# Queries and keys of one map side by side: three pairs of digit operations per tile in place of six

## The chip, the cores and the metric

The kernel runs on 1 core of one Trainium2 chip. The metric is the device time of one execution in microseconds (us), as the median of several runs. Engines are named as in the profile: PE (TensorE's matmuls), PEld (its weight loads), DVE (VectorE), ACT (ScalarE), POOL (GpSimd), SP (SyncE, which issues most DMAs).

## The reference, cut to what matters

One encoder layer on 1024 tokens of width 1024, in float32. The part that the change touches is the differential attention: 8 heads, and in each head two softmax maps (the index `i`), each with its own queries and keys of width 64, over one value of width 128.

```python
z = h @ w_in[l]
q = z[..., POOL_DIM:POOL_DIM + QK_DIM].reshape(B, S, N_HEADS, 2, HEAD_DIM)
k = z[..., POOL_DIM + QK_DIM:POOL_DIM + 2 * QK_DIM].reshape(B, S, N_HEADS, 2, HEAD_DIM)
...
qn = head_rmsnorm(q, g_q) * (HEAD_DIM ** -0.5)
kn = head_rmsnorm(k, g_k)
...
    s = jnp.einsum('bqhid,bkhid->bihqk', qblk, kn)
...
    s = jnp.where(allowed, s + bias, neg)
    p = jax.nn.softmax(s, axis=-1)
    a = p[:, 0] - lam * p[:, 1]
    return jnp.einsum('bhqk,bkhe->bqhe', a, vf)
```

Around it stand a pooling mixer, two sigmoid gates from `h @ w_gate`, an output projection and a squared-ReLU MLP.

## The kernel before, in words

**Digits.** Every float32 operand of a matmul is split into two: a high digit, which is the value rounded to the matmul's float32r format, and a low digit, the remainder. `split` (L117) writes the high one with an ACT copy (L119) and the low one with a DVE or POOL subtraction (L120). `mm3` (L122) then makes three matmuls of a product: high by high (L125), high by low (L126), low by high (L127).

**Stages of the attention.** The work is cut by head h (8) and tile t of 128 tokens (8), so in 64 steps. For each step the code writes these stages:

- A, `stage_qkv`: 24 matmuls into `z`, 128 tokens by q (128 columns), k (128), v (128).
- B, `stage_prep`: squares (ACT, L422), their sums (DVE, L423), the power -0.5 (POOL, L234), the values' digits, the normalized q and k in `qn` (DVE, L427), and the gains on the key part (POOL, L433).
- C, `stage_qkT`: two transposes of `qn` on PE into the bank `tk`, then the digits of K and Q. For each map ACT copies the high digit of K (L454), DVE subtracts for the low one (L455), ACT copies the high digit of Q (L456), DVE subtracts twice (L457, L458), ACT copies once more (L459). High digits of a map lie on its own 64 partitions, low digits on the other 64, so that one matmul over 128 partitions adds two digit products.
- D, `stage_scores`: for each map two matmuls `sc` per 512 keys (L485, L486), the bias and running minimum on DVE (L488), the exponential on ACT (L496), then the difference of the two maps on DVE (L503 to L505).
- E, `stage_aT`: transposes `ta` of the result (L541) and their digits `AT`. F, `stage_pv`: the products `po` with the values. H, `stage_ssq`: the sums of squares of the output, by two matmuls (L576, L577). R, `stage_norm`: row factors of the head, with a transpose `trr` (L597).

**Fill.** The gates (`gate_cols`, 16 column blocks c of 2 halves, matmuls `g`) and the pooling mixer (`pool_group`, 4 groups of 2 halves, matmuls `u` and `yp`) don't depend on the attention and are written to stand among it. A half of a gate is 24 matmuls into one bank; ACT then moves the bank to memory (L731; for `u` L696, for `yp` L723).

**Banks.** PSUM has 8 banks, all in use: 2 for `z`, 2 for `sc`, 2 shared by `tk`, `ta` and `trr`, 1 for `po`, and 1, the pool `ps_f`, for the fill. Fill tiles thus follow each other in one bank, and the next can't start before ACT has emptied the last. Only from gate column 13 on (`G_Z`) does `spare_bank` take the two `z` banks too.

**What sets the order.** Each engine runs its own list of instructions in order. The lists are made when the kernel is built, by a scheduler that goes by the order of the code (the string at L50 and the loop at L631 for the attention; the fill is written behind it and has lower priority) and by its own model of how long each instruction takes. A change of shapes therefore changes the lists everywhere in the attention.

**After the attention** come the branch projections (`bp`, `baX`, `baY`), the output projection (`op`), the MLP's up side (`X`, `Y`, `Z`, `W`) and its down side (`Da`, `Db`).

Of the kernel before, what the change touches and what calls it, by code (L numbers as in the profile page):

```python
# [17 lines left out]
P = 128  # L18
# [39 lines left out]
def encoder_kernel(  # L58
# [215 lines left out]
    with ExitStack() as ph:  # L274
# [6 lines left out]
        def s1(shape, dt, name, tag, bufs=1):  # L281
            return sq_pool.tile(shape, dt, tag=tag, name=name, bufs=bufs)
# [133 lines left out]
        def stage_prep(h, t):  # L416
# [6 lines left out]
            nc.vector.tensor_reduce(ms, sq.rearrange("p (a b) -> p a b", a=4), axis=AX.X, op=ALU.add)  # L423
            rsq(ms, ms, 4, 1.0 / HD)
            split(V[th][:, t % 4, 0, :], V[th][:, t % 4, 1, :], z[:, 256:384])
            qn = s1([P, 4, HD], F32, f"qn{h}_{t}", "qn", N_QN)
            nc.vector.tensor_tensor(  # L427
                qn,
                z[:, 0:256].rearrange("p (a b) -> p a b", a=4),
                ms.unsqueeze(2).broadcast_to([P, 4, HD]),  # L430
                op=ALU.mult,
            )
            nc.gpsimd.tensor_tensor(  # L433
                qn[:, 2:4, :], qn[:, 2:4, :], ggh.unsqueeze(1).broadcast_to([P, 2, HD]), op=ALU.mult
            )
            st[h, t] = {"qn": qn}
            yield
# [1 line left out]
        def stage_qkT(h, t):  # L439

            th, c0 = t // 4, (t % 4) * P
            K, qn = KV[h][0][th], st[h, t]["qn"]
            tr = ps_t.tile([P, 512], F32, tag="tr", name=f"tk{h}_{t}")
            for i in range(2):
                nc.tensor.transpose(
                    tr[:, i * P : (i + 1) * P], qn[:, 2 * i : 2 * i + 2, :].rearrange("p a b -> p (a b)"), identf
                )
            Q = s1([P, 2, 2, P], F32R, f"Q{h}_{t}", "Q", N_Q)
            halves = (slice(0, HD), slice(HD, P))
            for m in range(2):  # L450
                own, other = halves[m], halves[1 - m]
                q, k = tr[own, 0:P], tr[own, P : 2 * P]
                k_hi, q_hi = K[own, m, c0 : c0 + P], Q[own, m, 0, :]
                nc.scalar.copy(k_hi, k)  # L454
                nc.vector.tensor_tensor(K[other, m, c0 : c0 + P], k, f(k_hi), op=ALU.subtract)  # L455
                nc.scalar.copy(q_hi, q)  # L456
                nc.vector.tensor_tensor(Q[other, m, 0, :], q, f(q_hi), op=ALU.subtract)  # L457
                nc.vector.tensor_tensor(Q[own, m, 1, :], q, f(q_hi), op=ALU.subtract)  # L458
                nc.scalar.copy(Q[other, m, 1, :], q)  # L459
            st[h, t]["Q"] = Q  # L460
            yield

# [1066 lines left out]
```

## Time and profile before

| | |
|---|---|
| median of 3 runs | 1535.6 us (1534.63 to 1535.61) |
| the profiled execution, its own time | 1535.99 us |
| its span, first to last instruction | 1534.0 us |
| PE busy | 1514.5 us, 99% |
| DVE, ACT, POOL busy | 69%, 54%, 21% |
| granted TensorE clock | 1.00 |
| attention, first `tk` to last `po` matmul | about 43 to 690 us |

The page of the profile sums each engine's busy time; a window gives the same for a stretch of the span. A line of the timeline is start, duration, engine, line of the code, operation and operands, and in brackets the idle time of the engine before it with what ended it. Matmuls are pipelined: a 128x512 matmul is shown with some 0.39 us, but the next one starts 0.23 us after it.

### The profile page before, as it was taken

To read this page: it belongs to the slowest core of one execution; us is meant where nothing else is said; L and a number is where in the kernel's file an instruction comes from. 1 tells how busy PE (TensorE), PEld (TensorE's weight loads), DVE (VectorE), ACT (ScalarE), POOL (GpSimd) and SP (SyncE) were. 2 spreads that over 40 slices of the span, in tenths; PEclk is the share of its full clock that TensorE was granted. 3 is DMA by queue.
4 is the path that set the end of the run, shared out by engine and by line. 5 is a ranking of instruction groups with operands and counts; after the bars stand their busy time and mean duration, and the time that the engine had idled before them with its cause. 6 is when DMAs were issued, how large, how long until landed. Compare 5 with 4: busy or idle time off the path is not lost.

```text
span 1534.0 us, 22224 instructions
## 1 busy us (share of the span) xinstructions
PE 1514.5 (99%) x7601; PEld 1311.1 (85%) x7601; DVE 1063.2 (69%) x2358; ACT 825.3 (54%) x1821; POOL 329.4 (21%) x476
## 2 busy tenths in 40 slices
PE   7999999999999999999999999999999999999999
PEld 6999999899999999888888888888888888888887
DVE  6777776777778887845578549766665668556572
ACT  6666565656566566554465456565555634333331
POOL 6654563333334243312000111000000000000000
PEclk9999999999999999999999999999999999999999
DMA  7331321110202021626466634454333799537760
GB/s 243 112 119 52 107 95 57 53 60 31 83 23 90 17 77 63 240 76 242 149 199 215 225 111 137 166 184 158 138 138 110 256 357 372 179 124 260 226 193 28
DMA packets 171611, 221.11 MB, mean 144 GB/s; under 512 B 10901, under 2 KB 104810, under 8 KB 171498
## 3 DMA queue, kind: packets, MB, share of 16 engines
q1 hardware_dynamic: 154090, 192.39, 38.0%
q10 hardware_dynamic: 17408, 27.30, 4.8%
q8 instruction: 60, 0.98, 0.3%
q14 instruction: 53, 0.43, 0.1%
HBM read 157.76 MB, written 61.90 MB: 143 GB/s over the span
## 4 chain that ended last, share of the span: by engine, by line
PE 92%; DVE 3%; DMA 3%; SPq 1%; issue 1%; ACT 1%; POOL 0%; DVEq 0%; ACTq 0%
PE z L125 5%; PE z L127 5%; PE z L126 5%; PE Da L125 4%; PE Da L126 4%; PE Da L127 4%; PE g L125 3%; PE g L127 3%; PE g L126 3%; PE Db L126 3%; PE Db L125 3%; PE Db L127 3%; PE X L127 3%; PE X L126 3%; PE X L125 3%; PE sc L485 2%
## 5 line engine op out<-in xcount | busy, mean ns | idle before, releaser
L125 PE MATMUL z<-wqkv,hT 128*128 128x384 f32 x512 | 174.5, 341 | 0.1
L126 PE MATMUL z<-wqkv,hT 128*128 128x384 f32 x512 | 174.0, 340 | 0.0
L127 PE MATMUL z<-wqkv,hT 128*128 128x384 f32 x512 | 173.8, 340 | 0.0
L496 ACT ACTIVATE s<-s,nm 128x256 f32<-128x256 f32 (+7 forms) x128 | 99.7, 779 | 77.0 <-DVE nm L488 69.2
L125 PE MATMUL g<-hT,fwgate 128*128 128x512 f32 x256 | 100.8, 394 | 0.9 <-ACT go L731 0.9
L126 PE MATMUL g<-hT,fwgate 128*128 128x512 f32 x256 | 100.6, 393 | 0.0
L127 PE MATMUL g<-hT,fwgate 128*128 128x512 f32 x256 | 100.3, 393 | 0.0
L125 PEld LDWEIGHTS z<-wqkv,hT 128*128 128x128 f32 x512 | 96.6, 189 | 3.6 <-DVE qn L427 0.3
L126 PEld LDWEIGHTS z<-wqkv,hT 128*128 128x128 f32 x512 | 96.7, 189 | 3.2
L127 PEld LDWEIGHTS z<-wqkv,hT 128*128 128x128 f32 x512 | 96.6, 189 | 2.4 <-DVE hT L120 0.5
L234 POOL TENSOR_TENSOR ms<-ms,mhalf 128x4 f32<-128x4 f32 x64 | 67.4, 1053 | 128.7 <-DVE ms L233 113.5
L488 DVE CUSTOM_DVE_ANT_0 s<-sc,dist 128x512 f32<-128x512 f32 (+3 forms) x128 | 74.8, 585 | 13.4 <-PE sc L486 11.4
L120 DVE TENSOR_TENSOR AS<-s,AS 128x512 fp32r<-128x512 f32 x64 | 44.1, 692 | 35.8 <-ACT AS L119 35.7
L485 PE MATMUL sc<-K,Q 128*128 128x512 f32 (+2 forms) x192 | 67.2, 359 | 0.3 <-DVE nm L488 0.3
L120 POOL TENSOR_TENSOR wqkv<-rqkv,wqkv 128x384 fp32r<-128x384 f32 x60 | 62.6, 1057 | 13.1 <-ACT wqkv L119 9.7
L486 PE MATMUL sc<-K,Q 128*128 128x512 f32 (+2 forms) x192 | 65.1, 353 | 0.0
L459 ACT CAST Q<-tk 64x128 fp32r<-64x128 f32 x128 | 33.3, 260 | 50.7 <-DVE Q L458 48.4
L456 ACT CAST Q<-tk 64x128 fp32r<-64x128 f32 x128 | 33.2, 259 | 50.8 <-DVE K L455 49.4
L433 POOL TENSOR_TENSOR qn<-qn,ggh 128x128 f32<-128x128 f32 x64 | 31.4, 491 | 115.4 <-DVE qn L427 88.6
L125 PEld LDWEIGHTS g<-hT,fwgate 128*128 128x128 f32 x256 | 48.1, 188 | 9.3 <-ACT go L731 1.5
L127 PEld LDWEIGHTS g<-hT,fwgate 128*128 128x128 f32 x256 | 48.1, 188 | 8.8
L126 PEld LDWEIGHTS g<-hT,fwgate 128*128 128x128 f32 x256 | 48.1, 188 | 8.2
(475 smaller groups left out, 4651.8 us busy)
## 6 DMA issues: line engine op xcount, KB each, us to landing
wd<-in_w_down_dram SPq DMA_DIRECT2D x56, 512.0 KB, 5.9
wu<-in_w_up_dram SPq DMA_DIRECT2D x32, 512.0 KB, 4.5
udS<-us SPq DMA_DIRECT2D x64, 256.0 KB, 2.4
ur<-udS SPq DMA_DIRECT2D x32, 512.0 KB, 3.5
rqkv<-in_w_in_dram SPq DMA_DIRECT2D x64, 192.0 KB, 2.9
ud<-u ACTq DMA_DIRECT2D x48, 256.0 KB, 4.3
ur<-ud SPq DMA_DIRECT2D x24, 512.0 KB, 4.8
frgate<-in_w_gate_dram SPq DMA_DIRECT2D x32, 256.0 KB, 2.9
```

The lines of the kernel that those rows point to most:

```text
L120: return (lo_eng or nc.vector).tensor_tensor(lo, src, f(hi), op=ALU.subtract)
L125: nc.tensor.matmul(ps, lhs_hi, rhs_hi, start=first, stop=False, **kw)
L126: nc.tensor.matmul(ps, lhs_hi, rhs_lo, start=False, stop=False, **kw)
L127: nc.tensor.matmul(ps, lhs_lo, rhs_hi, start=False, stop=last, **kw)
L234: nc.gpsimd.tensor_tensor(dst, dst, mhalf[:, :n], op=ALU.pow)
L433: nc.gpsimd.tensor_tensor(qn[:, 2:4, :], qn[:, 2:4, :], ggh.unsqueeze(1).broadcast_to([P, 2, HD]), op=ALU.mult)
L456: nc.scalar.copy(q_hi, q)
L459: nc.scalar.copy(Q[other, m, 1, :], q)
L485: nc.tensor.matmul(dst, Q[:, i, 0, :], rhs, start=True, stop=False)
L486: nc.tensor.matmul(dst, Q[:, i, 1, :], rhs, start=False, stop=True)
L488: nc.vector.tensor_tensor_reduce(out=s[i][:, c : c + w], in0=sc[:, 0:w], in1=dist[:, o0 + c : o0 + c + w], scale=2.0 ** -(h + 1), scalar=B ...
L496: nc.scalar.activation(s[i][:, 0:n], s[i][:, 0:n], AF.Exp, bias=last, scale=-1.0, accum_out=Z[:, i, t : t + 1])
```

## The change

In `stage_prep` the normalized tile `qn` is laid out map by map: q of map 0, k of map 0, q of map 1, k of map 1 (before: both q, then both k). The operation that writes it and the POOL operation with the gains go over the same elements with other strides. In `stage_qkT` a transpose then gives one map with q on partitions 0 to 63 and k on 64 to 127, for both maps. So the digits of K of both maps are written by one ACT copy and one DVE subtraction, and those of Q by two of each. K's high digits lie on partitions 64 to 127, its low ones on 0 to 63; Q is laid out to match, with its two variants swapped. The number and the shapes of the matmuls stay.

```diff
-            qn = s1([P, 4, HD], F32, f"qn{h}_{t}", "qn", N_QN)
+            qn = s1([P, 2, 2, HD], F32, f"qn{h}_{t}", "qn", N_QN)
             nc.vector.tensor_tensor(
-                qn,
-                z[:, 0:256].rearrange("p (a b) -> p a b", a=4),
-                ms.unsqueeze(2).broadcast_to([P, 4, HD]),
+                qn.rearrange("p m a b -> p a m b"),
+                z[:, 0:256].rearrange("p (a m b) -> p a m b", a=2, m=2),
+                ms.rearrange("p (a m) -> p a m", a=2).unsqueeze(3).broadcast_to([P, 2, 2, HD]),
                 op=ALU.mult,
             )
             nc.gpsimd.tensor_tensor(
-                qn[:, 2:4, :], qn[:, 2:4, :], ggh.unsqueeze(1).broadcast_to([P, 2, HD]), op=ALU.mult
+                qn[:, :, 1, :], qn[:, :, 1, :], ggh.unsqueeze(1).broadcast_to([P, 2, HD]), op=ALU.mult
             )
...
-            for i in range(2):
+            for m in range(2):
                 nc.tensor.transpose(
-                    tr[:, i * P : (i + 1) * P], qn[:, 2 * i : 2 * i + 2, :].rearrange("p a b -> p (a b)"), identf
+                    tr[:, m * P : (m + 1) * P], qn[:, m, :, :].rearrange("p a b -> p (a b)"), identf
                 )
             Q = s1([P, 2, 2, P], F32R, f"Q{h}_{t}", "Q", N_Q)
-            halves = (slice(0, HD), slice(HD, P))
-            for m in range(2):
-                own, other = halves[m], halves[1 - m]
-                q, k = tr[own, 0:P], tr[own, P : 2 * P]
-                k_hi, q_hi = K[own, m, c0 : c0 + P], Q[own, m, 0, :]
-                nc.scalar.copy(k_hi, k)
-                nc.vector.tensor_tensor(K[other, m, c0 : c0 + P], k, f(k_hi), op=ALU.subtract)
-                nc.scalar.copy(q_hi, q)
-                nc.vector.tensor_tensor(Q[other, m, 0, :], q, f(q_hi), op=ALU.subtract)
-                nc.vector.tensor_tensor(Q[own, m, 1, :], q, f(q_hi), op=ALU.subtract)
-                nc.scalar.copy(Q[other, m, 1, :], q)
+            q, k = (tr[a * HD : (a + 1) * HD, 0 : 2 * P].rearrange("p (m c) -> p m c", m=2) for a in range(2))
+            at_q, at_k = slice(0, HD), slice(HD, P)
+            k_hi, q_hi = K[at_k, :, c0 : c0 + P], Q[at_q, :, 1, :]
+            nc.scalar.copy(k_hi, k)
+            nc.vector.tensor_tensor(K[at_q, :, c0 : c0 + P], k, f(k_hi), op=ALU.subtract)
+            nc.scalar.copy(q_hi, q)
+            nc.vector.tensor_tensor(Q[at_k, :, 1, :], q, f(q_hi), op=ALU.subtract)
+            nc.vector.tensor_tensor(Q[at_q, :, 0, :], q, f(q_hi), op=ALU.subtract)
+            nc.scalar.copy(Q[at_k, :, 0, :], q)
```

Because of the scheduler the lists of the engines change too. PE has 7603 instructions in both. The last attention matmul on PE, `trr7`, is row 3614 of 7257 rows of PE's list before and row 3421 of 7261 now (equal matmuls that follow each other make one row); behind that, apart from the order within the first branch projections (`bp`), PE's list is the same. Between `trr7` and `bp` stands the fill that is left over, more of it now. Three places, from the last head (7) on. In a row stand the line, the operation, the tile written with its head or column and its tile or half, the tiles read, and the shape.

PE, end of the half `u3_1` of the last pooling group, before:

```order
L126 MATMUL u3_1_8292<-hT3_1_1_337,fwpool3_1_8204 128x512
L127 MATMUL u3_1_8292<-hT3_1_0_336,fwpool3_1_8204 128x512
L125 MATMUL po6_3_6507<-AT6_3_4h_6293,V6_1_5261 128x256
L541 MATMUL ta7_0_0_6503<-identf_96,s7_0_6411 128x128
L126 MATMUL po6_3_6507<-AT6_3_4l_6294,V6_1_5261 128x256
L127 MATMUL po6_3_6507<-AT6_3_4h_6293,V6_1_5261 128x256
L125 MATMUL po6_3_6507<-AT6_3_4h_6293,V6_1_5261 128x256
```

and now:

```order
L539 MATMUL ta7_6_1_6653<-identf_96,s7_6_0_6570 128x128
L575 MATMUL po7_2_6627<-oqs7_2_6676,ones_103 128x256
L126 MATMUL u3_1_7908<-hT3_1_1_337,fwpool3_1_7820 128x512
L127 MATMUL u3_1_7908<-hT3_1_0_336,fwpool3_1_7820 128x512
L125 MATMUL g10_0_7960<-hT0_0_0_150,fwgate10_0_7952 128x512
L126 MATMUL g10_0_7960<-hT0_0_1_151,fwgate10_0_7952 128x512
```

Before, attention work of heads 6 and 7 stood behind `u3_1`; now the next tile of the same bank, gate half `g10_0`, stands directly behind it.

PE, from the first to the second half of gate column 11, before:

```order
L127 MATMUL g11_0_8417<-hT3_0_0_156,fwgate11_1_8414 128x512
L485 MATMUL sc7_5_1_512_6907<-K7_1_6098,Q7_5_6771 128x256
L486 MATMUL sc7_5_1_512_6907<-K7_1_6098,Q7_5_6771 128x256
L541 MATMUL ta7_4_0_6884<-identf_96,s7_4_0_6788 128x128 x4
L126 MATMUL po7_1_6891<-AT7_1_0l_6699,V7_0_6099 128x256
L127 MATMUL po7_1_6891<-AT7_1_0h_6698,V7_0_6099 128x256
```

and now:

```order
L126 MATMUL g11_0_8033<-hT3_0_1_157,fwgate11_1_8030 128x512
L127 MATMUL g11_0_8033<-hT3_0_0_156,fwgate11_1_8030 128x512
L595 MATMUL trr7_6742<-identf_96,r7_6735 8x128
L125 MATMUL g11_1_8061<-hT0_1_0_330,fwgate11_0_8025 128x512
L126 MATMUL g11_1_8061<-hT0_1_1_331,fwgate11_0_8025 128x512
```

Both halves use the one fill bank. Before, 17 attention matmuls stood between them, now one transpose.

ACT, around the copy of the mixed group 3, first half (`mix3_0`, which PE's `yp3_0` waits for), before:

```order
L496 ACTIVATE s6_6_1_6196,Z6_5262<-s6_6_1_6196,nm6_6_6197 128x896
L459 CAST Q6_7_6178<-tk6_7_6175 64x128
L119 CAST mix3_0_8254<-sum3_0_8_8248 128x512
L422 ACTIVATE sq7_2_6380<-z7_2_6311 128x256
L119 CAST V7_0_6099<-z7_2_6311 128x128
```

and now:

```order
L457 CAST Q7_7_6559<-tk7_7_6556 64x2x128
L729 ACTIVATE go9_1_7898<-g9_1_7873,cols_122 128x512
L119 CAST fwgate10_1_7957<-frgate10_1_7955 128x512
L119 CAST mix3_0_7870<-sum3_0_8_7864 128x512
L119 CAST AT7_2_0h_6501<-ta7_5_0_6577 128x4x128
```

The copy now stands behind the emptying of gate half `g9_1` (L729 is L731 of before). On PE, ten matmuls stand between the end of that half and the first matmul of `yp3_0`: two of 128x384, six transposes and two of 128x512.

## The prediction, on record before the result

> **What bounds the kernel now.** I read the page first, for who is busy; then windows over the attention, for whether PE waits there at all; then PE's waits by name, and the timeline at two of them.
>
> ```profile
> span 1534.0 us, 22224 instructions
> PE 1514.5 (99%) x7601; PEld 1311.1 (85%) x7601; DVE 1063.2 (69%) x2358; ACT 825.3 (54%) x1821; POOL 329.4 (21%) x476
> PE 92%; DVE 3%; DMA 3%; SPq 1%; issue 1%; ACT 1%; POOL 0%; DVEq 0%; ACTq 0%
> ```
>
> PE is busy 99% of the span, and 92% of the chain that ended last is PE. Time can fall only where PE waits, and it rises wherever PE is made to wait.
>
> ```profile
> 230.00:280.00 50.00, 48.27 (x282) 44.28 (x282) 36.02 (x116) 29.18 (x82) 16.78 (x24) 1.00 0.20 59
> 280.00:570.00 290.00, 290.00 (x1687) 268.06 (x1686) 227.39 (x730) 179.40 (x524) 112.12 (x162) 1.00 0.18 55
> 570.00:620.00 50.00, 50.00 (x296) 46.46 (x295) 39.84 (x125) 30.49 (x88) 21.13 (x26) 1.00 0.21 65
> 620.00:665.00 45.00, 43.69 (x222) 35.42 (x222) 36.86 (x92) 23.05 (x58) 9.41 (x14) 1.00 0.54 192
> ```
>
> After the stretch's bounds and length stand the busy times of PE, PEld, DVE, ACT and POOL, then the granted clock. From 280 to 620 us PE is busy for all of 340 us. It is idle for 1.73 us in the first of these windows and 1.31 us in the last, 3.04 us together. DVE is busy for 78% of the long window and ACT for 62%: they are the engines that the change relieves, and neither holds PE up there.
>
> ```profile
> PE ta L541 <- DVE AT_4l L120: 1.3, 1, 1.3
> PE g L125 <- ACT go L731: 0.9, 2, 0.5
> PE sc L485 <- DVE nm L488: 0.3, 1, 0.3
> PE yp L125 <- ACT go L731: 0.3, 1, 0.3
> ```
>
> These are all the waits of PE between 50 and 700 us: five, three of them for ACT to empty the fill bank. The idle time understates each, since a matmul's drawn end overlaps the next one:
>
> ```profile
> 233.15 0.33 PE L125 MATMUL z<-wqkv,hT 128*128 128x384 f32 x1
> 233.91 0.50 PE L125 MATMUL g<-hT,fwgate 128*128 128x512 f32 x1 [0.42 <-ACT go L731]
> 625.99 0.39 PE L125 MATMUL g<-hT,fwgate 128*128 128x512 f32 x1
> 631.24 0.39 PE L127 MATMUL g<-hT,fwgate 128*128 128x512 f32 x1
> ```
>
> The last two are the first and the last of a gate half's 24 matmuls: 5.25 us for 23 steps, a pitch of 0.228 us per 512 columns. By that a 128x384 matmul takes 0.17, a 128x256 one 0.11, a transpose of 128 columns 0.06 us (estimates by columns). The first two start 0.76 us apart, 0.17 of it the first one's own, so 0.59 us were lost where 0.42 is called idle, 0.17 more. With five such gaps the attention now loses 3.04 + 5 x 0.17 = 3.9 us to waits. That is all the change can win.
>
> **The operations themselves.**
>
> ```profile
> L455 DVE TENSOR_TENSOR K<-tk,K 64x128 fp32r<-64x128 f32 x128 | 36.9, 288 | 22.0 <-ACT K L454 18.5
> L457 DVE TENSOR_TENSOR Q<-tk,Q 64x128 fp32r<-64x128 f32 x128 | 36.9, 288 | 15.9 <-ACT Q L456 12.7
> L458 DVE TENSOR_TENSOR Q<-tk,Q 64x128 fp32r<-64x128 f32 x128 | 37.0, 289 | 2.9
> L454 ACT CAST K<-tk 64x128 fp32r<-64x128 f32 x128 | 33.2, 259 | 20.5 <-PE tk L445 17.5 <-issue 1.1
> L456 ACT CAST Q<-tk 64x128 fp32r<-64x128 f32 x128 | 33.2, 259 | 50.8 <-DVE K L455 49.4
> L459 ACT CAST Q<-tk 64x128 fp32r<-64x128 f32 x128 | 33.3, 260 | 50.7 <-DVE Q L458 48.4
> L427 DVE TENSOR_TENSOR qn<-z,ms 128x256 f32<-128x256 f32 x64 | 26.8, 419 | 18.9 <-PE tk L445 12.5 <-POOL ms L234 2.8 <-POOL wqkv L120 2.5
> L422 ACT ACTIVATE sq<-z 128x256 f32<-128x256 f32 x64 | 24.6, 384 | 8.4 <-PE z L127 7.6
> ```
>
> Each of the first six lines halves its count and doubles its columns. No 64x256 operation from PSUM is in the trace; I bound it by its own 64x128 time (no cost for columns) and twice that, and take the 128x256 rows L427 and L422, which have its length. DVE: 36.9 + 36.9 + 37.0 = 110.8 us become 192 x 0.419 = 80.4, 30 us less (55 to 0). ACT: 99.7 become 192 x 0.384 = 73.7, 26 us less (50 to 0). [...] On PE's path both are worth nothing, since the windows show PE not waiting for DVE or ACT beyond the 3.9 us. The chain from the transposes to K and Q becomes six steps in place of twelve; no row of PE's waits names K or Q, so that is worth nothing too. The strided write of `qn` (L427) and the strided POOL multiplication keep their sizes; I bound each by no change and by twice its time, 27 us more on DVE (L427) and less than POOL has free at 21% busy, and take no change. PE's 50 of 50 us hides it; where DVE is late for PE it would count in full, and that is the lateness allowed for below.
>
> **What it moves.** PE's work stays, but the lists pull the attention together: `trr7` stands 193 rows earlier, and the fill thus spared stands behind it. The old lists' five waits go with their places: I take all 3.9 us away. What is late next is where the attention's last tiles have too little fill among them and fill follows fill in one bank. The price of one hand-over of that bank:
>
> ```profile
> 639.42 0.39 PE L127 MATMUL g<-hT,fwgate 128*128 128x512 f32 x1
> 639.85 0.69 ACT L731 ACTIVATE go<-g,cols 128x512 f32<-128x512 f32 x1 [0.16 <-PE g L127]
> 632.51 0.69 ACT L731 ACTIVATE go<-g,cols 128x512 f32<-128x512 f32 x1
> 633.26 0.50 PE L125 MATMUL g<-hT,fwgate 128*128 128x512 f32 x1 [0.48 <-ACT go L731]
> L696 ACT COPY u<-u x8: 586/587/593, 313.3 to 603.3; 128x512 f32<-128x512 f32 x8
> ```
>
> The two pairs are the emptying at its earliest and what follows it. ACT starts 0.43 us after the start of the last matmul, takes 0.69 us (0.59 for `u`), and PE restarts 0.06 us after ACT's end (633.20 to 633.26): 1.18 us from start to start, 1.08 for `u`. PE's own pitch covers 0.23 of it and each matmul in between its own. Before, some 17 matmuls stood between; the lists now have places with hardly any. The other prices there:
>
> ```profile
> 604.92 0.39 ACT L565 ACTIVATE oq<-po 128x256 f32<-128x256 f32 x1
> 605.45 0.42 ACT L119 CAST oqs<-oq 128x256 fp32r<-128x256 f32 x1
> 644.49 0.43 DVE L120 TENSOR_TENSOR oqs<-oq,oqs 128x256 fp32r<-128x256 f32 x1
> 607.49 1.50 DVE L705 TENSOR_TENSOR sum<-sum 128x524 f32<-128x524 f32 x2
> 609.75 0.62 ACT L119 CAST mix<-sum 128x512 fp32r<-128x512 f32 x1 [0.88 <-DVE sum L714]
> L505 DVE SCALAR_TENSOR_TENSOR s<-s,cf,s 128x1024 f32<-128x1024 f32 x8 | 10.7, 1342 | 0.1
> L119 ACT CAST AT_0h<-ta 128x512 fp32r<-128x512 f32 x40 | 23.4, 585 | 2.1 <-PE ta L541 1.3 <-PE z L126 0.2
> L120 DVE TENSOR_TENSOR AT_0l<-ta,AT_0h 128x512 fp32r<-128x512 f32 x40 | 27.5, 688 | 9.2 <-ACT AT_0h L119 8.5
> ```
>
> The new waits, in PE's order:
>
> - `u3_0` to `g9_1`: two transposes between. 1.08 - 0.23 - 0.12 = 0.7 us.
> - `yp3_0`: ACT's copy of `mix3_0` stands behind the emptying of `g9_1` and a weight copy, so it ends 0.43 + 0.69 + 0.62 + 0.62 = 2.4 us after the last start of `g9_1`. PE has 0.23 + 2 x 0.17 + 6 x 0.06 + 2 x 0.23 = 1.4 us. 1.0 us.
> - `u3_1` to `g10_0`: nothing between. 1.08 - 0.23 = 0.85 us.
> - `ta7_7`: on DVE the mixed group's four sums and its scaling (5 x 0.75 us, each of 1.50 / 2) and a score step (taken as 0.75 too) stand ahead of the last head's difference (1.34): 5.8 us behind the copy of `u3_1`, against the 24 x 0.23 = 5.5 us of `g10_0`. 0.3 us if DVE does nothing else, 1.3 with two more such passes; I take 0.8.
> - `po7_3` right behind `ta7_7`: 0.43 + 0.59 + 0.69 = 1.7 us for the digits, against four transposes, three matmuls of `yp3_1` and one of `po`, 1.05 us. 0.65 us.
> - the sum of squares behind `po7_3`: 0.43, then 605.87 - 604.92 = 0.95 for square and high digits, 0.43 for the low ones, 1.8 us. Four matmuls of `g10_1` and two of 256 columns cover 1.1. 0.7 us, in which the bank's next hand-over (to `g11_0`) is hidden.
> - `g11_0` to `g11_1`: one transpose. 1.18 - 0.23 - 0.06 = 0.9 us.
> - scores: three hand-overs of the two score banks in tiles 4 to 7 of head 7 and one in head 4 are about as close as the one that cost 0.28 + 0.17 = 0.45 us before. 1.8 us.
>
> Sum: 0.7 + 1.0 + 0.85 + 0.8 + 0.65 + 0.7 + 0.9 + 1.8 = 7.4 us. ACT isn't always at its earliest: at 632.51 it began 1.27 us after the last gate matmul (631.24), 0.84 late. I allow that lateness once: 8.2 us. Against the 3.9 us that go, the sum is +4.3 us: 1535.99 + 4.3 = 1540.3 for the profiled execution, which lies 0.4 us above the median, so 1539.9 us, 0.3% slower. A measurement of this kernel can tell about 0.2%, 3.1 us.
>
> **The rivals.**
>
> *The waits do not add, and nothing changes.* While PE waits at one place, the other engines catch up for the next. It would happen in head 7's last four tiles: if the score waits, `g9_1` and `yp3_0` cost no more together than the largest of them (1.0 in place of about 1.3 + 0.7 + 1.0) and `ta7_7` and head 4 cost nothing, 2.0 + 0.8 + 0.5 + the 0.8 of lateness fall away, and 8.2 becomes 4.1: 1535.8 us. For it speaks that 340 us run without one wait now; against it that the waits for the single bank count from PE's own last matmul, so catching up does not shorten them. It decides from three of these gaps on that are not seen.
>
> *Faster.* DVE's 30 us and ACT's 26 us make the tail's chains end early, so the new places cost under 1 us, and the 3.9 us are won: about 1532.4 us. For it speaks that the list of waits holds no other; against it the fixed 1.18 us of a bank hand-over.
>
> *Much slower: the row factors.* On DVE's list, three scalings `ry` by row factors `rb` stand ahead of the low digits that the last sum of squares needs, and the two buffers of `rb` are only refilled when the mixing tiles and each other are done.
>
> ```profile
> DMA to landing us min/median/max: 3.5/3.5/3.5
> ```
>
> Two in a row behind `yp3_1` make 2 x (3.5 + 1.34) + 0.43 = 10.1 us, against 24 x 0.11 + 24 x 0.23 = 8.2 of PE: 1.9 us of wait in place of 0.7, 1541.1 us, within the forecast. It becomes a rival of its own if the wait grows to several us. The granted clock was 1.00 in the window with 1.73 us of idle. [...]
>
> *The change does not do what it says:* two blocks of 128 columns may cost as much as two operations. Then DVE keeps its 110.8 us, in lists that are made for less, and is late by up to 30 us where it can't catch up; above 1547 us.
>
> **How the numbers follow.** Forecast, slower by the new waits, 1538.7 to 1547: 0.52. Waits do not add, within 3.1 us of 1535.6: 0.32. Faster: 0.08. Clock: 0.04; no relief: 0.04. So slower 0.60, same 0.32, faster 0.08. The lower end is the second case with a little less (1535); the upper end takes every wait of the sum 0.84 us late (eight times, 6.7 us in place of 0.8, so 1545.8) and the row factors' 1.2 more. 1535 to 1547 leaves out about 2 in 10: most of the faster case, the low part of the unchanged one and the last two cases.
>
> **What would show it.** Right: DVE and ACT some 30 and 26 us less busy; `trr7` some 35 us earlier (193 rows at up to 0.23 us, less the waits); windows from 50 to 570 us with PE busy nearly throughout; PE's waits from there to `trr7` named `g`, `yp`, `ta`, `po` and `sc`, 0.3 to 1 us each, about 7 us together; no wait from there on to the branch projections. Wrong: fewer than 4 us of waits there (then the second or the third case), waits spread over all heads (lateness of DVE, no relief), a granted clock below 1.00, or 64x256 rows far from 0.42 and 0.38 us.

## The result, and the profile after

| | before | after |
|---|---|---|
| median of 6 runs each | 1535.61 us (1534.63 to 1536.92) | 1544.55 us (1543.69 to 1545.34) |
| the profiled execution, its own time | 1535.99 us | 1543.69 us |
| its span | 1534.0 us | 1541.8 us |

The ratio is 1.0057, with a 95% interval of 1.0045 to 1.007: the change makes the kernel 8.9 us slower. The forecast was 4.3 us slower, the top of its range 1547.

The page, the engines' busy times with their shares of the span:

```profile
span 1541.8 us, 21897 instructions
...
PE 1516.4 (98%) x7601; PEld 1312.4 (85%) x7601; DVE 1025.7 (67%) x2166; ACT 798.1 (52%) x1629; POOL 324.5 (21%) x476
```

DVE is 37.5 us less busy than before and ACT 27.2, and the span is 7.8 us longer. The digit operations and `qn` (L427) by line, with count, busy time in us and mean of one in ns:

```profile
L453 DVE TENSOR_TENSOR K<-tk,K 64x256 fp32r<-64x256 f32 x64 | 27.3, 426 | 11.9 <-ACT K L452 10.1
...
L427 DVE TENSOR_TENSOR qn<-z,ms 128x256 f32<-128x256 f32 x64 | 26.9, 420 | 26.8 <-PE tk L445 24.3 <-POOL ms L234 2.3
L455 DVE TENSOR_TENSOR Q<-tk,Q 64x256 fp32r<-64x256 f32 x64 | 26.8, 418 | 7.6 <-ACT Q L454 6.0
L456 DVE TENSOR_TENSOR Q<-tk,Q 64x256 fp32r<-64x256 f32 x64 | 26.7, 416 | 0.8
...
L452 ACT CAST K<-tk 64x256 fp32r<-64x256 f32 x64 | 23.5, 368 | 34.2 <-PE tk L445 33.2
L454 ACT CAST Q<-tk 64x256 fp32r<-64x256 f32 x64 | 23.4, 366 | 29.6 <-DVE K L453 29.2
L457 ACT CAST Q<-tk 64x256 fp32r<-64x256 f32 x64 | 23.3, 364 | 29.7 <-DVE Q L456 28.3
```

The three DVE lines of digits sum to 80.8 us (110.8 before), the three ACT lines to 70.2 (99.7 before): 30 and 29.5 us saved, and the strided `qn` costs what it did (0.420 against 0.419). So the operations do what they were expected to do. Where PE lost the time, by windows with the bounds of before (busy times in the order PE, PEld, DVE, ACT, POOL, then the granted clock):

```profile
230.00:280.00 50.00, 50.00 (x295) 46.26 (x294) 34.84 (x112) 27.02 (x71) 19.49 (x30) 1.00 0.18 62
280.00:570.00 290.00, 289.77 (x1703) 269.18 (x1702) 213.55 (x661) 171.03 (x442) 111.14 (x161) 1.00 0.17 53
570.00:620.00 50.00, 48.40 (x269) 42.14 (x267) 37.13 (x111) 30.50 (x76) 17.16 (x28) 1.00 0.35 121
620.00:665.00 45.00, 38.02 (x185) 30.52 (x184) 26.62 (x54) 15.57 (x32) 9.84 (x11) 0.96 0.47 146
665.00:700.00 35.00, 34.32 (x152) 28.08 (x151) 4.88 (x9) 14.35 (x24) 8.03 (x6) 1.00 0.32 106
```

From 230 to 570 us PE is idle for 0.23 us (before, it was 3.04 from 230 to 665). From 570 to 700 it is idle for 1.60 + 6.98 + 0.68 = 9.26 us, and in the worst of these windows the granted clock is 0.96. PE's waits there, by name:

```profile
PE po L575 <- DVE oqs L120: 3.4, 1, 3.4
PE ta L539 <- DVE s L503: 1.6, 1, 1.6
PE trr L595 <- POOL r L593: 1.0, 1, 1.0
PE ta L539 <- DVE sum L710: 1.0, 1, 1.0
...
PE g L125 <- ACT fwgate L119: 0.7, 1, 0.7
PE g L125 <- ACT u L694: 0.7, 1, 0.7
PE tk L445 <- DVE AT_0l L120: 0.6, 1, 0.6
```

The first is the longest: the second matmul of the last sum of squares waits for the low digits of the squares, `oqs7_3`. The timeline around it (start, duration, engine, line, operation; in brackets the idle time ahead of it):

```profile
647.89 1.28 DVE L198 SCALAR_TENSOR_TENSOR ry<-ry,gs,rb 128x1024 f32<-128x1024 f32 x1 [1.48 <-DMA rb<-r_dram]
...
649.14 0.42 ACT L119 CAST oqs<-oq 128x256 fp32r<-128x256 f32 x1
...
649.61 0.38 PE L574 MATMUL po<-oqs,ones 128*128 128x256 f32 x1
...
650.67 1.28 DVE L198 SCALAR_TENSOR_TENSOR ry<-ry,gs,rb 128x1024 f32<-128x1024 f32 x1 [1.49 <-DMA rb<-r_dram]
650.93 2.15 POOL L120 TENSOR_TENSOR fwgate<-frgate,fwgate 128x512 fp32r<-128x512 f32 x1 [3.36 <-ACT fwgate L119]
651.87 1.48 DVE L120 TENSOR_TENSOR oqs<-oq,oqs 128x256 fp32r<-128x256 f32 x1
...
653.41 0.58 PE L575 MATMUL po<-oqs,ones 128*128 128x256 f32 x1 [3.42 <-DVE oqs L120]
...
653.79 0.63 PE L125 MATMUL g<-hT,fwgate 128*128 128x512 f32 x1
...
654.22 0.63 PE L126 MATMUL g<-hT,fwgate 128*128 128x512 f32 x1
...
655.93 0.54 PE L127 MATMUL g<-hT,fwgate 128*128 128x512 f32 x1
...
656.31 0.39 PE L125 MATMUL g<-hT,fwgate 128*128 128x512 f32 x1
```

The high digits are ready at 649.56. DVE is free then, but next in its list stands the scaling `ry3`, and that waits until 650.67 for its row factors to land. When DVE comes to the low digits it takes 1.48 us for them in place of 0.42, until 653.35, beside a POOL subtraction that runs from 650.93 to 653.08. The two matmuls start 3.8 us apart in place of 0.12, and the gate matmuls behind them start 0.43 us apart in place of 0.23, until 656.31 (granted clock 0.51 from 653.40 to 656.31).

**The measure used below.** For each pair of matmuls that follow each other between 40 and 760 us I take the time from start to start, less the median for the first one's kind, and add up those over 0.12 us. By this "lost time" before lost 4.5 us and after 13.2. Span less lost time lies between 1527.1 and 1530.8 us in all 14 kernels of this study, so the lost time tells most of each difference, to within 3.7 us. What it leaves out are small losses: a 128x256 matmul at half rate, for one, loses 0.10 us (`e8`, 0.213 us from start to start in place of 0.116) and isn't counted.

### The profile page after: what moved, and what is told of

Same layout as the page of the kernel before. It is cut to its first block, busy times and chain, and to the rows that moved or that the text cites. A ratio compares the mean times of both kernels' runs of the same rounds, so it can differ in the third digit from the quotient of the medians.

```text
span 1541.8 us, 21897 instructions
## 1 busy us (share of the span) xinstructions
PE 1516.4 (98%) x7601; PEld 1312.4 (85%) x7601; DVE 1025.7 (67%) x2166; ACT 798.1 (52%) x1629; POOL 324.5 (21%) x476
## 4 chain that ended last, share of the span: by engine, by line
PE 54%; DVE 2%; DMA 2%; issue 0%; ACT 0%; SPq 0%; POOL 0%; ACTq 0%; DVEq 0%; POOLq 0%
PE Da L125 4%; PE Da L127 4%; PE Da L126 4%; PE Db L127 3%; PE Db L126 3%; PE Db L125 3%; PE X L127 3%; PE X L125 3%; PE X L126 3%; PE op L127 2%; PE op L126 2%; PE op L125 2%; PE Z L127 2%; PE Z L125 2%; PE Z L126 2%; PE g L125 1%
## 5 line engine op out<-in xcount | busy, mean ns | idle before, releaser
L483 PE MATMUL sc<-K,Q 128*128 128x512 f32 (+2 forms) x192 | 70.5, 370 | 0.2 <-DVE nm L486 0.2
L484 PE MATMUL sc<-K,Q 128*128 128x512 f32 (+2 forms) x192 | 65.9, 347 | 0.0
L120 POOL TENSOR_TENSOR fwgate<-frgate,fwgate 128x512 fp32r<-128x512 f32 x32 | 43.9, 1377 | 68.3 <-ACT fwgate L119 65.6
L125 PE MATMUL op<-wo,mT 128*128 128x512 f32 x128 | 50.5, 395 | 0.0
L126 PE MATMUL op<-wo,mT 128*128 128x512 f32 x128 | 50.1, 391 | 0.0
```

Of the source, the lines that this page charges most:

```text
L120: return (lo_eng or nc.vector).tensor_tensor(lo, src, f(hi), op=ALU.subtract)
L125: nc.tensor.matmul(ps, lhs_hi, rhs_hi, start=first, stop=False, **kw)
L126: nc.tensor.matmul(ps, lhs_hi, rhs_lo, start=False, stop=False, **kw)
L483: nc.tensor.matmul(dst, Q[:, i, 0, :], rhs, start=True, stop=False)
L484: nc.tensor.matmul(dst, Q[:, i, 1, :], rhs, start=False, stop=True)
```

## The experiments

**Theories.** *Order:* the new operations are only cheaper; the loss is in where the engines' lists now put things, above all the scalings by row factors (L198), of which four of six (`ry0` to `ry3`) are made in the 10 us right ahead of the last head's low digits; in the kernel before all six are done by 648.04 us, and the low digits of the last sum of squares come at 685.25. *Layout:* the new places or shapes of the operands make the steps slower. *Bank:* the loss is the fill in a single bank, which now stands at the end with nothing between. Times are medians; "over before" is against the kernel before, timed beside each group on the same chip (1535.19 us for `e1` to `e4`, 1536.01 for `e5` to `e8`, 1535.62 for `e9` to `e12`). "Lost" is the measure above, of the profiled execution.

| kernel | us | over before | ratio, 95% interval | lost |
|---|---|---|---|---|
| before | 1535.61 | | | 4.5 |
| after | 1544.55 | +8.9 | 1.0057 (1.0045 to 1.007) | 13.2 |
| `e1`, after, low digits ahead of the scalings | 1539.24 | +4.1 | 1.0024 (1.0013 to 1.0034) | 8.1 |
| `e2`, after, scalings and their casts out of the tail | 1538.61 | +3.4 | 1.0022 (1.0013 to 1.0031) | 7.9 |
| `e3`, after, three banks from column 9 | 1534.70 | -0.5 | 0.9996 (0.9988 to 1.0005) | 4.8 |
| `e8`, after, three banks from column 10 | 1534.72 | -1.3 | 0.9994 (0.9985 to 1.0003) | 4.2 |
| `e6`, `e2` and `e3` together | 1531.46 | -4.6 | 0.9972 (0.9962 to 0.9983) | 1.3 |
| `e4`, new layout, twelve operations | 1542.62 | +7.4 | 1.0048 (1.0035 to 1.006) | 9.8 |
| `e7`, `e4` with three banks from column 9 | 1552.21 | +16.2 | 1.0106 (1.0092 to 1.012) | 20.8 |
| `e5`, before, three banks from column 9 | 1552.58 | +16.6 | 1.0109 (1.0095 to 1.0123) | 20.5 |
| `e12`, before, scalings out of the tail | 1537.51 | +1.9 | 1.0013 (1.0004 to 1.0022) | 7.3 |
| `e9`, after, two digit operations issued twice | 1541.29 | +5.7 | 1.0035 (1.0023 to 1.0048) | 10.0 |
| `e10`, `e9` with three banks from column 9 | 1551.18 | +15.6 | 1.01 (1.0086 to 1.0113) | 19.8 |
| `e11`, keys map by map, three banks from column 9 | 1547.83 | +12.2 | 1.0077 (1.0063 to 1.0091) | 16.2 |

### e1 and e2: the scalings in VectorE's list

`issue_after(x)` puts what its block writes for the engine of x behind x in that engine's list. Line numbers in these two are up by 2.

```diff
-            split(oqs[:, 0, :], oqs[:, 1, :], oq)
+            stored["sq"] = split(oqs[:, 0, :], oqs[:, 1, :], oq).ins
...
-    for d in range(NK - 2):
-        yr[d] = y_scaled(d, row_factors(d))
+    with tc.issue_after(stored["sq"]):
+        for d in range(NK - 2):
+            yr[d] = y_scaled(d, row_factors(d))
```

> The changed kernel, with the six row-factor scalings (`ry0` to `ry5`, VectorE) held behind the low digits of the last head's squares (`oqs7_3`); nothing else is edited. Order theory: the new operations are cheaper and cost nothing, and most of the 8.9 us lie in where the scalings stand in VectorE's list, ahead of those low digits: the sum of squares lost 3.96 us and the gate matmuls behind it ran at half rate for about 1.2 us more. Of the 3.96 some 0.3 stay (the digits themselves), so 3.7 + 1.2 = 4.9 us go and the time is about 1539.7 (1538.7 to 1540.7 where the wait of `trr7`, 1.16 us, and of `fwgate13`, 0.84, stay; up to 3 more if `go11_1`, which now stands behind the high digits of `yb5`, is waited for). Layout theory: the normalization and the digits in their new places made each step of a head slower, and the late scalings are only where it shows: no more than 1 us goes, 1543.5 to 1544.6. Clock: if the half rate is a matter of the long wait, no matmul of this stretch is at half rate any more; if it comes from elsewhere it stays, and the time is about 1541.

Measured: 1539.24 us, 4.9 us nearer to before than the changed kernel, as the order theory said; the layout theory's 1543.5 falls. The place, DVE, POOL and PE:

```profile
648.49 1.29 POOL L120 TENSOR_TENSOR fwgate<-frgate,fwgate 128x512 fp32r<-128x512 f32 x1 [10.87 <-ACT fwgate L119]
648.75 1.32 DVE L120 TENSOR_TENSOR oqs<-oq,oqs 128x256 fp32r<-128x256 f32 x1 [6.54 <-ACT oqs L119]
...
650.02 0.28 PE L576 MATMUL po<-oqs,ones 128*128 128x256 f32 x1
650.13 0.37 PE L577 MATMUL po<-oqs,ones 128*128 128x256 f32 x1
```

The two matmuls now follow each other in 0.11 us, and no matmul behind them is at half rate (granted clock 1.00 from 620 to 665 us). Beside POOL the low digits still take 1.32 us, which PE's other matmuls cover. The waits at `trr7` and `fwgate13`, which I had left in, are gone too; three hand-overs of the fill bank of 0.7 to 0.9 us stand there in their place.

In the second one the scalings go behind the row factors' last VectorE step and the casts of the scaled rows behind the last gate eviction:

```diff
+            stored["r"] = nc.vector.tensor_scalar(r, r, 1.0 / P, EPS, ...).ins
...
+    with tc.issue_after(stored["r"]):
         for d in range(NK - 2):
...
+            with tc.issue_after(stored["go"]):
                 split_b(d - 3)
```

> The changed kernel, with the row-factor scalings `ry0` to `ry5` held behind the last VectorE step of the last head's row factors (`r7`), and the high digits `yb` of the scaled rows (ScalarE) held behind the last eviction of the gate fill; both are first needed at about 755 us. Order theory: all four losses that the two lists cause go: 3.7 of 3.96 at the sum of squares, 1.2 of half rate, 1.16 at `trr7`, 0.84 at gate column 13: 6.9 us, so about 1537.7 (1537 to 1538.5), and what is left above the kernel before, about 2 us, is the hand-overs of the single fill bank (0.84) and `ta7_7` (1.79) less what before lost there. Layout theory: 1543.5 to 1544.6, as the steps of the heads stay as slow as they are. Third theory, that a stall only moves: the time falls by less than 3 us and a new wait of several us stands between 650 and 700 us.

Measured: 1538.61 us, 5.5 us nearer to before. The forecast of 6.9 was 1.4 too much: taking more away than in `e1` gained 0.6 us, which the intervals of the two can't tell from nothing. The trace loses 0.71, 0.87 and 0.49 us where a gate matmul waits for ACT to empty a bank (650, 657 and 685 us). They stood behind the longer waits. For this part the third theory was right in kind, a stall that only moves, though the time fell by more than the 3 us it allowed and no new wait reaches 1 us.

### e3 and e8: banks for the fill

```diff
-G_FIRST, G_Z = 13, 13
+G_FIRST, G_Z = 13, 9
```

> The changed kernel, with the gate columns from 9 on (in place of 13) taking the two banks of the projections besides the fill's single one (`G_Z` 9). This moves the fill's place in TensorE's list too: columns 9 and 10 then stand partly ahead of `u3_1`. Bank theory: the hand-overs of the single bank are the main loss, and a tail with three banks lets gate matmuls run while VectorE is late: 4 us or more go, 1540.5 or less. Order theory: the bank's own share is the 0.84 us at `g10_0` and perhaps half of the 1.79 at `ta7_7`; the scalings still stand ahead of the low digits of `oqs7_3` (three of them and one sum), so the long wait stays unless gate matmuls now stand between: 1542.5 to 1544.

Measured: 1534.70 us, no difference from before, and 9.4 us nearer to it than the changed kernel. The order theory's 1542.5 falls, and the time is as the bank theory said, though PE's list moved with the setting. PE still waits for the low digits, 2.2 us, and 1.0 us for `trr7`; the losses at `tk7_7`, `ta7_5`, `g10_0`, `ta7_7` and `fwgate13` (0.77, 1.16, 0.84, 1.79, 0.84 us) are gone.

With 10 in place of 9:

> The changed kernel with the gate columns from 10 on in three banks (`G_Z` 10, between 13 and 9). In its list the low digits of `oqs7_3` already stand ahead of all six scalings, and `trr7` in row 3467 (3421 with 13, 3502 with 9). Order theory: the long wait of 3.7 us and the half rate of 1.2 behind it are gone by the list alone, and so is `g10_0` behind `u3_1` (0.84); the waits of `tk7_7` (0.77) and `ta7_5` (1.16), earlier than column 10, stay, and `trr7` may stay (1.16): 1544.55 - 5.7 = about 1538.8 (1537 to 1540). Bank theory alone (the gain goes with the number of fill columns that have three banks): a little less than half way or more, about 1537 to 1539 as well. They part on the place: by the order theory the record shows no wait over 1 us at the sum of squares, by the bank theory it does.

Measured: 1534.72 us, 2.3 us below the lower end of both. On the place the order theory was right: no wait stands at the sum of squares. But `ta7_5` and `trr7` are gone as well, and a new wait of 1.60 + 0.61 us stands at the start of `po7_3`. Both theories sized this list wrongly: one number moves it in more places than either followed.

### e4 and e7: the layout alone

The transposes, `qn` and the halves of the partitions as in the changed kernel, and the loop over the maps as before:

```diff
-            q, k = (tr[a * HD : (a + 1) * HD, 0 : 2 * P].rearrange("p (m c) -> p m c", m=2) for a in range(2))
-            k_hi, q_hi = K[at_k, :, c0 : c0 + P], Q[at_q, :, 1, :]
+            for m in range(2):
+                q, k = (tr[a * HD : (a + 1) * HD, m * P : (m + 1) * P] for a in range(2))
+                k_hi, q_hi = K[at_k, m, c0 : c0 + P], Q[at_q, m, 1, :]
...
```

> The layout of the changed kernel alone: queries and keys normalized side by side per map, digits of both maps on the same half of the partitions, but written map by map, by twelve operations of 64x128 in place of six of 64x256, as many as before the change. Order theory: with as many operations as before the lists come out nearly as before (the scalings stand ahead of the last head's scores again, `trr7` in row 3586 of TensorE's list against 3614 before and 3421 after), so the time is that of before within 1.5 us: 1535 to 1537. Layout theory: the new places cost, and so the time stays above 1541.

Measured: 1542.62 us, against my expectation of 1535 to 1537, on the layout theory's side. Its operations cost what they did before (64x128: 0.283 to 0.293 us on DVE, 0.258 to 0.262 on ACT; `qn` 0.418). What it loses, 9.8 us, it loses at other places than before or after: 1.34 us at a sum of squares (558 us), 1.58 at a score that waits for `Q` behind an exponential in ACT's list (630), 1.73 at another sum of squares (641), and 0.2 to 0.9 at a dozen more.

The same with `G_Z` 9:

> The layout of the changed kernel with twelve operations, map by map, and gate columns from 9 on in three banks. With the single bank this layout took 1542.6, and TensorE lost 9.8 us in it, at other places than in the changed kernel: 558, 585, 627, 639 and 648 us. Order theory: these losses come from this one list, and another list of the same operations loses another amount, nearer to what the kernel before loses with three banks: 1534 to 1538. Layout theory: the same operations cost the same 7 us again, about 1542.

Measured: 1552.21 us, far above both. But it is what the old layout took with the same bank setting (1552.58, `e5` below): at twelve operations and three banks the layouts differ by 0.4 us. So the layout theory, by which the new layout costs 7 us wherever it stands, falls with `e7`, and the order theory's expectation that any other list loses less falls too.

### e5 and e12: the same edits in the kernel before

With `G_Z` 9:

> The kernel before the change, with the gate columns from 9 on taking the two banks of the projections besides the single one (`G_Z` 9 in place of 13). Before lost 0.59, 0.44 and 0.64 us on TensorE at hand-overs of the single bank (233, 622 and 632 us). Bank theory (three banks help because the quicker heads of the changed kernel leave the fill short of banks): the kernel before gains at most the two late ones, 1.1 us, and loses as much where the scalings now stand ahead of the low digits of `oqs7_3`, as they do in its new list: 1534 to 1537. Setting theory (9 is simply the better number, whatever the operations): it gains as much as the changed kernel did, 5 us or more, 1530 or less.

Measured: 1552.58 us, 16.6 over before: the number that takes 9.4 us from the changed kernel adds 16.6 to the old one. Neither theory had that. The window from 530 to 620 us, first of `e5` and then of `e3`, which has the same setting (DVE's busy time is the third):

```profile
530.00:620.00 90.00, 81.06 (x459) 73.12 (x457) 72.66 (x243) 53.38 (x165) 30.66 (x44) 0.96 0.21 71
```

```profile
530.00:620.00 90.00, 90.00 (x506) 80.85 (x505) 66.99 (x200) 51.09 (x128) 28.55 (x44) 1.00 0.23 79
```

With the old operations PE is idle for 8.9 of 90 us there while DVE is busy for 81%; with the new ones PE isn't idle and DVE is busy for 74%. The longest wait in `e5`, on DVE and PE:

```profile
545.18 1.60 DVE L505 SCALAR_TENSOR_TENSOR s<-s,cf 128x512 f32<-128x512 f32 x1
...
546.81 0.29 DVE L455 TENSOR_TENSOR K<-tk,K 64x128 fp32r<-64x128 f32 x1
...
547.13 0.69 DVE L488 CUSTOM_DVE_ANT_0 s<-sc,dist 128x512 f32<-128x512 f32 x1
...
548.37 0.29 DVE L457 TENSOR_TENSOR Q<-tk,Q 64x128 fp32r<-64x128 f32 x1
...
548.72 0.63 PE L485 MATMUL sc<-K,Q 128*128 128x512 f32 x2 [2.16 <-DVE Q L457]
```

The scores wait for the low digits of `Q`, which stand behind a difference of 1.60 us, the low digits of `K` and two score passes in DVE's list. Here, and not in the list of before, the digits of K and Q are on PE's path: in `e5` PE waits 4.0 us for `Q` from L457 alone, in three places.

With the edit of `e2`:

> The kernel before the change with the row-factor scalings and the high digits of the scaled rows held behind the last head's row factors and the last gate eviction, as in the second experiment. Before has its scalings at rows 1501 to 1559 of VectorE's list, ahead of the last scores, and no wait of over 0.7 us from 570 to 700 us. Order theory: there is nothing to take away there, so 1535 to 1537; the edit that gave the changed kernel 5.9 us gives the kernel before nothing. Theory that the late scalings are better for any list: 1533 or less.

Measured: 1537.51 us, 1.9 over before. Nothing was gained, as the order theory said; that it would lose a little, 0.5 us beyond the theory's range, was not expected. The profiled execution (1538.87 us) lost 1.74 us at a transpose at 637 us and some 1.6 us in the matmuls at half rate behind it (0.43 us apart from 638.21 on, granted clock 0.96 from 620 to 665 us).

### e9, e10 and e11: how much of the relief the three banks need

Here the changed kernel issues the last DVE subtraction and the last ACT copy of each tile twice (`e9`; with three banks `e10`); in `e11` the keys' digits are written map by map.

```diff
-            nc.vector.tensor_tensor(Q[at_q, :, 0, :], q, f(q_hi), op=ALU.subtract)
-            nc.scalar.copy(Q[at_k, :, 0, :], q)
+            for _ in range(2):
+                nc.vector.tensor_tensor(Q[at_q, :, 0, :], q, f(q_hi), op=ALU.subtract)
+                nc.scalar.copy(Q[at_k, :, 0, :], q)
```

> The changed kernel (single fill bank up to column 12) with two of its six digit operations issued twice: the low digits of the queries on VectorE and the copy behind them on ScalarE, so that a tile costs 4 x 0.418 = 1.67 us on VectorE (before 6 x 0.288 = 1.73, after 1.26) and 4 x 0.366 = 1.46 on ScalarE (before 1.55, after 1.10). Load theory: where the lists put things follows from how much VectorE and ScalarE have to do, so the list comes out like one of twelve operations (`trr7` in row 3661 against 3614 before, 3586 map by map, 3421 after) and the time is what such a list happens to lose: 1534 to 1543, not above the changed kernel's 1544.55. Operation theory (the 64x256 operations themselves are what is slow): slower than 1544.55 by some us more, 1546 or over.

Measured: 1541.29 us, within the load theory's wide range and below the changed kernel, although each tile has two operations more: the repeat costs nothing that can be seen beside what the new list changes, and the operation theory falls.

> The same two operations issued twice, and gate columns from 9 on in three banks. With three banks, twelve operations took 1552.6 (before) and 1552.2 (map by map), six took 1534.7. Load theory: what the three banks need is the time that VectorE and ScalarE no longer spend, so with the load nearly back the time is nearly back too: 1545 to 1555. Count theory: it is the shorter chain from one operation to the next (six in place of twelve) that helps, and two repeats take back a third of it: 1535 to 1541.

Measured: 1551.18 us, as the load theory said. Against before, the repeats take the changed kernel from +8.9 to +5.7 with one bank, and from -0.5 to +15.6 with three. The record of `e10` shows one way by which the banks bring DVE's load to PE. From column 9 on the fill shares the two `z` banks with the projections, and a `z` bank comes free only when DVE, among others, has read it (for `qn`). But for the wait at the start, the two largest rows of PE's waits in `e10` are these, of the projections (`z`) and of a gate half (`g`); the list of `e3` has neither:

```profile
PE z L125 <- DVE qn L427: 2.6, 3, 1.7
PE g L125 <- DVE qn L427: 2.2, 1, 2.2
```

```diff
-            nc.scalar.copy(k_hi, k)
-            nc.vector.tensor_tensor(K[at_q, :, c0 : c0 + P], k, f(k_hi), op=ALU.subtract)
+            for m in range(2):
+                nc.scalar.copy(k_hi[:, m, :], k[:, m, :])
+                nc.vector.tensor_tensor(K[at_q, m, c0 : c0 + P], k[:, m, :], f(k_hi[:, m, :]), op=ALU.subtract)
```

> The changed kernel with the keys' digits written map by map (two pairs of 64x128 operations in place of one pair of 64x256), the queries' in one, and gate columns from 9 on in three banks: 2 x 0.288 + 2 x 0.418 = 1.41 us of VectorE and 2 x 0.26 + 2 x 0.366 = 1.25 us of ScalarE a tile. Load theory: between six operations (1.26 us, 1534.7) and twelve (1.73, 1552.6), on the side of six: 1535 to 1543. Threshold: if the load only matters from where the lists turn late, 1534 to 1536.

Measured: 1547.83 us, above the load theory's 1543, and the threshold theory falls clearly. With three banks the times are in the order of DVE's time per tile, 1.26 us (1534.7), 1.41 (1547.8), 1.67 (1551.2), 1.73 (1552.6), but not in proportion: the first third of the way brings three quarters of the loss. ACT's time per tile has the same order (1.10, 1.25, 1.46 and 1.55 us), and each kernel has its own list, so these runs don't tell which of the two engines it is, nor what part is the list's. With one bank there is no such order: 1.26 us (1544.6), 1.67 (1541.3), 1.73 (1542.6 in the new layout, 1535.6 in the old).

### e6: both edits together

> The changed kernel with both edits: gate columns from 9 on in three banks, and the row-factor scalings and the high digits of the scaled rows behind the last head's row factors and the last gate eviction. With three banks alone the changed kernel took 1534.7, and TensorE still lost 2.32 us at the sum of squares of `po7_3` (low digits of `oqs7_3` late) and 1.17 us at `trr7`. Order theory: both go, down to some 0.4 at the sum of squares: about 1531.6 (1531 to 1533), below the kernel before by 3 us or more. Theory that a stall only moves: 1534 or more.

Measured: 1531.46 us, as the order theory said, and 4.6 us faster than the kernel before (ratio 0.9972, 0.9962 to 0.9983). All rows of PE's waits in its record but the first, of the start of the kernel:

```profile
PE X L127 <- DVE A L120: 0.9, 1, 0.9
PE Y L125 <- DVE u L1248: 0.8, 1, 0.8
PE Da L125 <- DVE u L1248: 0.5, 1, 0.5
PE z L127 <- DVE hT L120: 0.2, 1, 0.2
PE sc L485 <- DVE nm L488: 0.2, 1, 0.2
PE po L126 <- DVE AT_0l L120: 0.2, 1, 0.2
```

In the attention 0.2 us is the longest that is left, and the first three belong to the MLP and stand in the records of before and after too.

## Why the prediction was right and where it was wrong

The direction and the mechanism were right: the operations save what the 128x256 rows said (30 and 26 us forecast, 30 and 29.5 measured), none of it reaches PE, the lists pull the attention together (`trr7` starts at 661.5 us in place of 699.4, 38 us earlier against some 35), and new waits at its end cost more than the old five did. The size was off: the forecast was 4.3 us, and 8.9 were measured, inside the range since its upper end allowed for lateness at every wait and for the row factors. Of the signs that the prediction gave for being wrong one came, a granted clock below 1.00 (0.96 from 620 to 665 us), and its list of PE's waits came only in part: two waits are over 1 us (3.4 and 1.6), `tk` and `trr` wait too, and one wait stands behind `trr7`. Term by term, in us of lost time:

| term | forecast | measured |
|---|---|---|
| `u3_0` to `g9_1` | 0.7 | 0.77, but at `tk7_7` between them, behind low digits on DVE |
| `yp3_0` | 1.0 | 0; `ta7_5`, ahead of it, waits 1.16 behind the pooling sums |
| `u3_1` to `g10_0` | 0.85 | 0.84 |
| `ta7_7` | 0.8 | 1.79 |
| `po7_3` behind it | 0.65 | 0.31 |
| last sum of squares | 0.7 | 0.28 + 3.68 = 3.96 |
| half rate behind it | not in the sum | 1.41 |
| `g11_0` to `g11_1` | 0.9 | 0; `trr7` between them waits 1.16 for POOL |
| gate column 13 | not seen | 0.84, its cast behind the casts of the scaled rows |
| scores, and the projections after them | 1.8 | 0.71, at 384 and 485 us, none in the last head |
| lateness | 0.8 | within the above |
| sum | 8.2 | 12.95 |
| before's waits | 3.9 | 4.3 |

- **The step that failed is the price of the last sum of squares.** The sum of the prediction took 0.7 us for it, from the digits alone, and left the row factors to a rival that priced it at 1.9 us; 3.96 were measured. The rival had the right chain, two scalings in a row behind `yp3_1`, each behind the landing of its row factors (four scalings stand ahead of the low digits, where the prediction counted three, but `ry1` and `ry3`, which share a buffer, set the time). It had the terms too small: 2 x (3.5 + 1.34) + 0.43 = 10.1 us. In the trace the row factors of `ry1` are issued at 640.76 and land at 645.11; those of `ry3` are issued at 646.45, as soon as `ry1` is done, and land at 650.65; the low digits end at 653.35. That is 12.6 us. Of the 2.5 us more, 1.55 lie in the two landings, 4.35 and 4.20 us in place of the 3.5 that the kernel before showed, and 1.05 in the low digits, which take 1.48 us beside POOL and not 0.43; the scalings took 0.1 less. Why the landings are slower here was not tried. DVE stands idle for these landings, 1.48 and 1.49 us in the rows above. Behind the wait comes the half rate, 1.41 us (granted clock 0.51 from 653.40 to 656.31 us). The 0.04 that I had given the clock rested on no row of the kernel before, whose granted clock was 1.00 throughout. The sum of squares and the half rate together are 4.7 us over their forecast, a little more than the whole difference between the 12.95 - 4.3 = 8.65 us of lost time measured and the 4.3 forecast. `e1` shows it: with the low digits ahead, 4.9 us go.
- **The other terms came out right in their sum, not each in its place:** 7.5 us forecast without the sum of squares, 7.6 measured. That the two sums agree so closely is luck. Two of the hand-overs that I priced were hidden behind a longer wait for DVE or POOL, and DVE's waits were longer. As the third theory of `e2` showed, such waits stand behind one another: where one goes, the next hand-over shows.
- **"Waits do not add"** had 0.32. It holds in part (the hidden hand-overs above), but it needed new waits of 4.1 us together, and 12.95 were measured.
- **"DVE's relief is worth nothing on PE's path"** is nearly true of the lists of before and after, with one bank for the fill: up to 570 us PE loses 2.1 us in waits before and 0.7 after. As a statement about the operations it is wrong. With three banks from column 9 the six operations take 1534.7 us and the twelve 1552.2 in the same layout and 1552.6 in the old one: there the same relief, with the lists that come with it, is worth some 17 us. The prediction read the value of a relief from one list and could not have seen this; the digits lie on PE's path in the lists of `e5` (4.0 us for `Q`) and, once, of `e4` (1.58 us), and not in those that it had.
- **No relief and faster:** excluded by the rows of the operations and by the result.

**What stays open.** Each kernel has its own list, made by the scheduler. I have no pair with the same list and different operations, so I can't separate what a list loses because of its order from what it loses because the chip is slower than the scheduler's model at the time. That matters for `e4`: 7 us over before with as many operations of the same lengths, all of it in waits, but why that list is worse than the one of before was not tried. That the list of before is simply a good one among several is argued, not shown.

## What to carry to other kernels

Where a scheduler places the work, a change of shapes is two changes: the operations, which can be priced from rows, and a new list, which can cost more than they save. Look in the new list for what now stands ahead of the last step of the longest chain, price every DMA landing (4.20 and 4.35 us here) and every operation that runs beside POOL (1.48 us here in place of 0.42) in front of it, and move low-priority work behind it: here such a move and another bank setting together turned 8.9 us slower into 4.6 us faster. A setting that was tuned for the old operations (here the column from which the fill gets more banks) has to be tried again with the new ones, since it can differ in sign.

## What the runs showed of the hardware that was not expected

**VectorE and GpSimd operations took longer side by side.** In the changed kernel the subtraction of `oqs7_3` takes 1.48 us in place of 0.42 and ends some 0.28 us after the POOL subtraction that started ahead of it (653.35 and 653.08); in `e1` it takes 1.32 and ends as long after it (650.07 and 649.78). Nine other lengthened ones of this shape (0.64 to 1.32 us), in the traces of before and after, end some 0.28 us after a POOL instruction that started ahead of them too. The other way round, the POOL subtraction of the changed kernel started 0.26 us behind the scaling `ry3` and took 2.15 us, where the median of its kind is 1.29. Over the heads of the changed kernel the operation takes, shortest, median and longest in ns:

```profile
L120 DVE TENSOR_TENSOR oqs<-oq,oqs x32: 406/424/1484, 73.5 to 651.9; 128x256 fp32r<-128x256 f32 x32
```

Why the two operations take longer was not tried.

**Half rate stood behind a wait of 1.58 us and not behind one of 2.15.** In the changed kernel the half rate follows 3.42 us of idle time. In `e12` it follows this:

```profile
635.32 0.28 PE L488 MATMUL sc<-K,Q 128*128 128x256 f32 x1
...
637.18 0.33 PE L543 MATMUL ta<-identf,s 128*128 128x128 f32 x1 [1.58 <-DVE AT_0l L120]
...
637.59 0.50 PE L125 MATMUL g<-hT,fwgate 128*128 128x512 f32 x1
...
638.21 0.63 PE L127 MATMUL g<-hT,fwgate 128*128 128x512 f32 x1
...
638.64 0.63 PE L125 MATMUL g<-hT,fwgate 128*128 128x512 f32 x1
```

The idle time is 1.58 us, then come a transpose and, 0.41 us after its start, the first gate matmul; from 638.21 on the gate matmuls start 0.43 us apart. In `e5` the granted clock is 0.96 from 530 to 620 us, the stretch with the wait of 2.16 us shown above. In `e3` no half rate stands behind a wait of 2.15 us, and the granted clock is 1.00 from 620 to 665 us:

```profile
658.65 0.40 PE L126 MATMUL g<-hT,fwgate 128*128 128x512 f32 x1
...
661.20 0.39 PE L575 MATMUL po<-oqs,ones 128*128 128x256 f32 x1 [2.15 <-DVE oqs L120]
...
661.42 0.40 PE L127 MATMUL g<-hT,fwgate 128*128 128x512 f32 x1
```

The length of one wait doesn't decide it here. What decides was not tried.
